# Three 32-byte offsets and the last operations of a streaming-encoder trunk

## The chip, the cores and the metric

The kernel runs on one core of one Trainium2 chip. The metric is the device time of one execution in microseconds (us). Times of several runs are given as a median; the trace is that of one profiled execution, whose own time stands beside its span below.

## What is computed

One layer of a trunk over 512 tokens of width 1024, all in float32. Four parallel mixers (a spatially gated MLP, gated linear attention, chunked attention, a convolution module) read one normalised input; each is projected and gated, and their sum is projected and added to the stream. A squared-ReLU MLP of width 4096 follows, and then the part which the tail of the kernel computes:

```python
def rms_norm(x, g):
    xf = x.astype(jnp.float32)
    y = xf * lax.rsqrt(jnp.mean(xf * xf, axis=-1, keepdims=True) + EPS)
    return (y * g.astype(jnp.float32)).astype(x.dtype)
...
        hg = rms_norm(h, norm3_g[i])
        ple_gate = jax.nn.sigmoid(jnp.einsum('bsd,de->bse', hg, w_ple_gate[i]) + b_ple_gate[i])
        h = h + ple_gate * jnp.einsum('bsq,qd->bsd', p[i], w_ple[i])
    return rms_norm(h, final_g)
```

The last norm has two factors for each element: one for its token (the reciprocal root, `rms` below) and one for its channel (`final_g`, `rowp[2]` and `rowp[3]` below).

## The kernel before

**Matmuls.** Every matrix product is written as three float32r products: each operand is split into a high and a low part (ScalarE copies the high part, VectorE subtracts), and high by high, low by high and high by low are added in PSUM. Weights come in pieces of 128 x 1024 numbers (`raw`, and `grow` for sums of pieces), are split into `wh` and `wl` (line 173 and 186 through `split_piece`), and are used by `ch_mm`, `tok_mm` or `product`, which all go through `mm` (line 191). One matmul reads a moving operand of 512 columns, while the next one's stationary operand of 128 columns is loaded. In the profile's names `b<-x,wh` the moving tile stands first and the stationary one second.

**Where tiles lie.** The order of all engines' work is the order of the program's text (`manual_schedule`). Memory of a partition is given out by pools that are stacked one behind the other. In a pool, a name with several buffers takes that many slots, in order of first use, and each slot is rounded up to 32 bytes. Pool `sb` is first and stays to the end. It begins at byte 16512, which is 0 modulo 64: `ident`, `later`, `jp`, `mean` (512 bytes each), `ind` (8 bytes, a slot of 32), `ones` (4, a slot of 32), `mhalf` (64), `vecs` (784 bytes, a slot of 800, which is 32 modulo 64). So everything that follows, from byte 19488 on, lies at 32 modulo 64 (and 32 modulo 128): `h`, `raw`, `wh`, `wl`, `x`, `v`, in slots that are multiples of 256 bytes together with the small ones between them. `sq3` (32 bytes) is asked for late, is the last of the pool, and brings its end to 133696, which is 0 modulo 64 (64 modulo 128). There the second pool begins: `early` (the tiles `u`, `stack`, `pad0` to `pad3`), and in its place later `late` (`grow`, `ht`, `act`, `combo`, `z`, `s1`, `s3`). All their tiles lie at 0 modulo 64. The `x`, `h`, `wh` and `wl` which matmuls read lie below byte 126240, and all tiles of the second pool above 133696.

Which pairs a matmul reads: input projections and gates read `x` with `wh`/`wl` (one pool). The first projections (up to 62 us), the branch products of three of the mixers and the output projection read `u` with `wh`/`wl` (two pools). The second half of the MLP reads `combo` with `wh`/`wl` (two pools), and its first half `x` (one pool). The attention scores read `stack` with `stack` (one pool, the second).

**The tail.** `ht[tb, half]` holds the stream: four blocks of 128 tokens, two halves of 512 channels. `gate(tb, half, b)` is one VectorE operation on the PSUM bank (norm factor, bias) and a tanh on ScalarE. `embed(tb, half)` is two VectorE operations (gate times embedding, then half of it added to `ht`) and a Square with a sum on ScalarE; `add_sum` (one small VectorE operation) adds its sum to the token's mean. `power` (line 369) raises to the power -0.5 on GpSimd. For each block, `first_part` lets GpSimd multiply half 0 by `rowp[2]` (line 1238), the evacuation lets GpSimd multiply half 1 by `rowp[3]` (line 1285), and `write` multiplies both halves by `rms[tb]`, on ScalarE (line 186) or for the later blocks on VectorE (line 182), and sends each half from the SP queue (line 1248). TensorE runs the second half's products block by block (24 matmuls of 512 columns); block 3 comes as two groups of 256 columns. The evacuation of block tb stands, in each engine's order, behind the products of block tb and ahead of the evacuation of block tb + 1.

Of the kernel before, what the change touches and what calls it, by code (L numbers as in the profile page):

```python
# [41 lines left out]
FILL = 0.72  # L42
WARM = 4
E_SLOTS = 28

# [83 lines left out]
def build(tc, x, w, vec, wa2, sgw, rows, rb, pt, out):  # L131
# [15 lines left out]
    def U(dt=F32):  # L147
        return epool.tile([128, 512], dt, tag="u", bufs=E_SLOTS, name=name("u"))

# [29 lines left out]
    def ts(o, a, s1, s2, op0, op1=None):  # L179
        cost["dve"] += 60 + 0.55 * size(o)  # L180
        if op1 is None:
            return DVE.tensor_scalar(o, a, s1, None, op0=op0)
        return DVE.tensor_scalar(o, a, s1, s2, op0=op0, op1=op1)  # L183

    def copy(o, a, **k):
        return ACT.activation(o, a, AF.Copy, **k)  # L186
# [34 lines left out]
    ones = gpool.tile([128, 1], F32, name="ones")  # L221
    mhalf = gpool.tile([128, 16], F32, name="mhalf")
    vecs = gpool.tile([128, NVEC], F32, name="vecs")
    warm = U()


# [84 lines left out]
    def step(last, mms, evac, own=True, lead=LEAD):  # L311

        prefetch(last, 0)
        now[0] = (last, lead)
        advance()
        b = bank() if own else None
        mms(b)
        fill()
        if evac is not None:
            evac(b)  # L320
        return b
# [36 lines left out]
    def tok_mm(o, j, i, tb, xk, nw, first, last, c0=0, cn=None):  # L358

        hi, lo = parts[j]  # L360
        c = slice(i * nw + c0, i * nw + c0 + (cn or nw))
        t = slice(tb * 128, tb * 128 + 128)
        mm(o, xk[0][:, t], hi[:, c], first, False)
        mm(o, xk[0][:, t], lo[:, c], False, False)
        mm(o, xk[1][:, t], hi[:, c], False, last)

    def power(ms, n):
        r = small(n)
        POOL.tensor_tensor(r, ms, mhalf[:, :n], op=OP.pow)  # L369
        return r  # L370
# [453 lines left out]
    for m in range(2):  # L824
        def evac(b):
            t = H()
            copy(t, b, scale=0.125)
            gq.append(t)
# [332 lines left out]
            transpose(b[:, tb * 128:tb * 128 + 128], ht[tb, k // 4][:, (k % 4) * 128:(k % 4) * 128 + 128])  # L1161
        hg3[k] = scaled_split(b, col("n3", k))

    sq3 = gpool.tile([128, 2, 4], F32, name="sq3")

    def squares(half):
        for tb in range(4):
# [48 lines left out]
    def gate(tb, half, b, c=slice(0, 512)):  # L1216
        z = zs[tb, half] = zt[half][:, tb, c]
        stt(z, b[:, c], rn["n3"][:, tb:tb + 1], rowp[half][:, c], OP.mult, OP.add)
        ACT.activation(z, z, AF.Tanh, scale=0.5)

    def embed(tb, half, c=slice(0, 512)):

        z = zs.pop((tb, half))
        stt(z, z, 1.0, ups[tb, half][:, c], OP.add, OP.mult)
        h = ht[tb, half][:, c]
        stt(h, z, 0.5, h, OP.mult, OP.add)
        a = small(1)
        ACT.activation(z, h, AF.Square, accum_out=a)  # L1228
        return a

    def add_sum(tb, a):
        e = small(1)
        ts(e, a, 1.0 / D, sums.get(tb, EPS), OP.mult, OP.add)
        sums[tb] = e

    def first_part(tb):
        a = embed(tb, 0)
        POOL.tensor_tensor(ht[tb, 0], ht[tb, 0], rowp[2], op=OP.mult)  # L1238
        add_sum(tb, a)

    def write(tb):
        for i in (1, 0):
            o = ht[tb, i]
            if i and tb >= 2:
                ts(o, o, rms[tb], None, OP.mult)
            else:
                copy(o, o, scale=rms[tb])
            nc.sync.dma_start(out[0, tb * 128:tb * 128 + 128, i * 512:i * 512 + 512], o)

    rms = {}  # L1250
    late_k = (4, 5, 6, 7, 0, 1, 2, 3)

    def channels():
# [7 lines left out]
    for i in range(4):  # L1261
        def mms(_, i=i):
            for q in range(2):
                if q:
                    middle()
                for tb in range(4):
                    tok_mm(bs[tb], base["ple0"] + i, q, tb, hg3[late_k[2 * i + q]], 512, i + q == 0, i + q == 4 and q == 1)

        step(base["ple0"] + i, mms, None, own=False, lead=4)
    for tb in range(4):  # L1270
        gate(tb, 0, bs[tb])
    first_part(0)
    for tb in range(4):
        def mms(b, tb=tb):
            for k in range(NKD):
                tok_mm(b, base["ple1"] + k // 2, k % 2, tb, hg3[late_k[k]], 512, k == 0, k == NKD - 1)

        def evac(b, tb=tb):
            gate(tb, 1, b)
            if tb:  # L1280
                write(tb - 1)
            first_part(tb + 1)
            add_sum(tb, embed(tb, 1))
            rms[tb] = power(sums[tb], 1)
            POOL.tensor_tensor(ht[tb, 1], ht[tb, 1], rowp[3], op=OP.mult)  # L1285

        if tb < 3:
            step(base["ple1"] + 3, mms, evac)
    for c in (0, 256):
        b = bank()  # L1290
        for k in range(NKD):
            tok_mm(b[:, c:c + 256], base["ple1"] + k // 2, k % 2, 3, hg3[late_k[k]], 512, k == 0, k == NKD - 1, c,
                   256)
        cs = slice(c, c + 256)
        gate(3, 1, b, cs)
        if c:
            write(2)
            tt(ht[3, 1][:, 0:256], ht[3, 1][:, 0:256], rowp[3][:, 0:256], OP.mult)
        add_sum(3, embed(3, 1, cs))
    rms[3] = power(sums[3], 1)  # L1300
    tt(ht[3, 1][:, 256:512], ht[3, 1][:, 256:512], rowp[3][:, 256:512], OP.mult)
    write(3)
    ctx.close()


# [60 lines left out]
```

## Time and profile before

| | us |
|---|---|
| median of 3 runs | 1006.32 (1005.86 to 1007.16) |
| the profiled execution's own time | 1004.86 |
| its span in the trace | 1002.9 |
| TensorE busy in the span | 981.5 (98%) |
| VectorE busy | 661.6 (66%) |
| ScalarE busy | 412.0 (41%) |
| GpSimd busy | 86.7 (9%) |

The span runs from the first to the last recorded instruction; the own time has 1.96 us around it. TensorE's matmuls are pipelined: the profile models their ends, so that two neighbours overlap, and what counts is the time from one start to the next. In a row that merges n instructions, start to start is (the row's length less the length of one) divided by n - 1. "Idle before" is time in which an engine had nothing to run, with what ended it.

### The profile page before, as it was taken

How to read it: one execution, taken by the hardware profiler on the slowest of the kernel's cores; microseconds unless marked ns; L12 is line 12 of the kernel's file. 1: busy time of each engine (PE TensorE's matmuls, PEld its weight loads, DVE VectorE, ACT ScalarE, POOL GpSimd, SP SyncE). 2: the span in 40 equal slices, each digit the busy share in tenths (PEclk: the TensorE clock that was granted, in tenths of full speed). 3: DMA queues.
4: the chain of work that ended last, by engine and by line, in shares of the span. 5: the costliest groups of instructions: out<-in, count | busy, mean ns of one | idle time of the engine just before them, and what ended most of it. 6: DMA issues, size and time to landing. Idle time of an engine off the chain costs nothing.

```text
span 1002.9 us, 11777 instructions
## 1 busy us (share of the span) xinstructions
PE 981.5 (98%) x4550; PEld 805.9 (80%) x4550; DVE 661.6 (66%) x917; ACT 412.0 (41%) x615; POOL 86.7 (9%) x94
## 2 busy tenths in 40 slices
PE   8999999999999999999999999999999999999993
PEld 6978888887888888888888888888888888877882
DVE  7746896487888987555444543575575587578565
ACT  6554764223323232324333434444434334335633
POOL 5001000001001500000000000020011011001012
PEclk9999999999999999999999999999999999999997
DMA  6334331322242223223252242464566459568202
GB/s 237 129 109 141 97 95 64 106 96 73 92 144 101 98 74 123 65 83 126 90 171 96 84 147 70 120 141 132 168 149 187 126 151 232 168 152 221 84 1 84
DMA packets 36595, 121.02 MB, mean 121 GB/s; under 512 B 4123, under 2 KB 4284, under 8 KB 36540
## 3 DMA queue, kind: packets, MB, share of 16 engines
q1 hardware_dynamic: 31292, 101.40, 30.2%
q0 software_dynamic: 5248, 18.88, 10.2%
q8 instruction: 36, 0.59, 0.2%
q14 instruction: 19, 0.16, 0.0%
HBM read 116.07 MB, written 2.10 MB: 118 GB/s over the span
## 4 chain that ended last, share of the span: by engine, by line
PE 92%; DVE 3%; issue 2%; ACT 1%; POOL 1%; DMA 1%; SPq 0%; POOLq 0%; DVEq 0%; ACTq 0%
PE b L191 90%; PE b L195 2%; DVE wl L173 1%; DVE ht L173 1%; DMA stack<-stack 0%; POOL ht L1285 0%; DMA raw<-w 0%; DVE s L173 0%; ACT ht L186 0%; ACT combo L186 0%; DVE z L177 0%; ACT z L1228 0%; POOL ht L1238 0%; POOL s L369 0%; DVE ht L177 0%
## 5 line engine op out<-in xcount | busy, mean ns | idle before, releaser
L191 PE MATMUL b<-x,wh 128*128 128x512 f32 x1440 | 361.2, 392 | 0.0
L191 PEld LDWEIGHTS b<-x,wh 128*128 128x128 f32 x1440 | 267.9, 188 | 56.7 <-issue 1.2
L173 DVE TENSOR_TENSOR wl<-raw,wh 128x1024 fp32r<-128x1024 f32 (+2 forms) x166 | 202.5, 1235 | 47.8 <-ACT wh L186 46.6
L191 PE MATMUL b<-x,wl 128*128 128x512 f32 x720 | 192.8, 389 | 0.0
L186 ACT ACTIVATE wh<-raw 128x1024 fp32r<-128x1024 f32 (+2 forms) x166 | 169.3, 1041 | 24.7 <-PE b L191 19.5
L191 PEld LDWEIGHTS b<-x,wl 128*128 128x128 f32 x720 | 135.2, 188 | 28.2
L191 PE MATMUL b<-wh,combo 128*128 128x512 f32 x448 | 144.5, 396 | 0.5 <-DVE ht L173 0.5
L191 PEld LDWEIGHTS b<-wh,combo 128*128 128x128 f32 x448 | 84.1, 188 | 20.7 <-issue 0.9
L191 PE MATMUL b<-wl,combo 128*128 128x512 f32 x224 | 88.8, 397 | 0.3 <-DVE wl L173 0.3
L177 DVE SCALAR_TENSOR_TENSOR u<-pad,vecs,u 128x512 f32<-128x512 f32 x120 | 86.2, 780 | 0.0
L191 PE MATMUL b<-u,wh 128*128 128x512 f32 x320 | 85.4, 396 | 0.0
L1005 ACT ACTIVATE act<-act 128x512 f32<-128x512 f32 x32 | 20.2, 633 | 150.9 <-DVE act L177 150.9
L191 PEld LDWEIGHTS b<-u,wh 128*128 128x128 f32 x320 | 59.8, 188 | 14.5 <-issue 0.3
L177 DVE SCALAR_TENSOR_TENSOR u<-u,b 128x512 f32<-128x512 f32 x36 | 24.7, 685 | 68.7 <-PE b L191 64.3
L191 PE MATMUL b<-wh,x 128*128 128x512 f32 (+1 forms) x208 | 60.8, 374 | 0.0
L857 ACT ACTIVATE u<-b,vecs 128x512 f32<-128x512 f32 x32 | 22.0, 686 | 90.3 <-PE b L191 90.3
L177 DVE SCALAR_TENSOR_TENSOR act<-b,v 128x512 f32<-128x512 f32 x32 | 22.0, 691 | 55.8 <-PE b L191 55.4
L191 PE MATMUL b<-wh,u 128*128 128x512 f32 (+1 forms) x192 | 53.5, 362 | 1.2 <-ACT wh L186 1.2
L369 POOL TENSOR_TENSOR s<-s,mhalf 128x4 f32<-128x4 f32 (+1 forms) x16 | 15.4, 965 | 441.7 <-DVE s L183 321.6
L191 PEld LDWEIGHTS b<-wl,combo 128*128 128x128 f32 x224 | 42.1, 188 | 11.4 <-DVE wl L173 1.5
L191 PE MATMUL b<-u,wl 128*128 128x512 f32 x160 | 47.7, 395 | 0.0
L191 PEld LDWEIGHTS b<-wh,x 128*128 128x128 f32 x208 | 38.1, 188 | 6.9
(171 smaller groups left out, 1029.7 us busy)
## 6 DMA issues: line engine op xcount, KB each, us to landing
raw<-w SPq DMA_DIRECT2D x161, 512.0 KB, 3.4
grow<-w POOLq DMA_DIRECT2D x24, 512.0 KB, 7.8
h<-x SPq DMA_DIRECT2D x16, 256.0 KB, 5.2
grow<-w SPq DMA_DIRECT2D x8, 512.0 KB, 4.7
raw<-w POOLq DMA_DIRECT2D x8, 512.0 KB, 6.9
v<-rb SPq DMA_DIRECT2D x8, 256.0 KB, 4.3
stack<-stack POOLq DMA_DIRECT2D x8, 256.0 KB, 3.8
out<-ht SPq DMA_DIRECT2D x8, 256.0 KB, 2.1
```

The lines of the kernel that those rows point to most:

```text
L173: return DVE.tensor_tensor(o, a, b, op=op)
L177: return DVE.scalar_tensor_tensor(o, a, s, b, op0=op0, op1=op1)
L186: return ACT.activation(o, a, AF.Copy, **k)
L191: PE.matmul(o, l, r, start=start, stop=stop, **k)
L195: PE.transpose(o, i, ident)
L369: POOL.tensor_tensor(r, ms, mhalf[:, :n], op=OP.pow)
L857: ACT.activation(th, gb, AF.Tanh, scale=0.5, bias=col("bg", n * 8 + m))
L1005: ACT.activation(a, a, AF.Square)
```

## The change

Two tiles of pool `sb` are asked for right behind `vecs`: `sq3`, which was the pool's last, and a new `pad` of 32 bytes that nothing uses. With `sq3` behind `vecs` the next byte is 0 modulo 64, with the pad 32 modulo 64: the large tiles of `sb` now begin at 19552, and the pool ends at 133728. Both are 32 modulo 64 (and 96 modulo 128), so all tiles of all pools that matmuls read have one offset.

In the tail no product by `rowp` is left on GpSimd. For blocks 0 to 2, `finish` multiplies by the token's factor and by the channel's in one VectorE operation and sends. For block 3, `gained` multiplies half 0 and the first 256 columns of half 1 by the channel's factor on VectorE ahead of the sum, ScalarE multiplies these by the token's, and the last 256 columns go through the one VectorE operation. The embedding of half 0 of block tb + 1 moves ahead of the evacuation of block tb, and the power stands right behind the last sum. Both 256-column groups of block 3 stand, in TensorE's order, ahead of all evacuation of block 3. There are nine output transfers in place of eight.

```diff
--- before.py
+++ after.py
@@ -42,6 +42,7 @@
 FILL = 0.72
 WARM = 4
 E_SLOTS = 28
+PAD = 8
 
 
 
@@ -221,6 +222,8 @@
     ones = gpool.tile([128, 1], F32, name="ones")
     mhalf = gpool.tile([128, 16], F32, name="mhalf")
     vecs = gpool.tile([128, NVEC], F32, name="vecs")
+    sq3 = gpool.tile([128, 2, 4], F32, name="sq3")
+    gpool.tile([128, PAD], F32, name="pad")
     warm = U()
 
 
@@ -1161,7 +1164,6 @@
             transpose(b[:, tb * 128:tb * 128 + 128], ht[tb, k // 4][:, (k % 4) * 128:(k % 4) * 128 + 128])
         hg3[k] = scaled_split(b, col("n3", k))
 
-    sq3 = gpool.tile([128, 2, 4], F32, name="sq3")
 
     def squares(half):
         for tb in range(4):
@@ -1228,26 +1230,30 @@
         ACT.activation(z, h, AF.Square, accum_out=a)
         return a
 
-    def add_sum(tb, a):
+    rms = {}
+
+    def add_sum(tb, a, last=False):
         e = small(1)
         ts(e, a, 1.0 / D, sums.get(tb, EPS), OP.mult, OP.add)
         sums[tb] = e
-
-    def first_part(tb):
-        a = embed(tb, 0)
-        POOL.tensor_tensor(ht[tb, 0], ht[tb, 0], rowp[2], op=OP.mult)
-        add_sum(tb, a)
-
-    def write(tb):
-        for i in (1, 0):
-            o = ht[tb, i]
-            if i and tb >= 2:
-                ts(o, o, rms[tb], None, OP.mult)
-            else:
-                copy(o, o, scale=rms[tb])
-            nc.sync.dma_start(out[0, tb * 128:tb * 128 + 128, i * 512:i * 512 + 512], o)
-
-    rms = {}
+        if last:
+            rms[tb] = power(e, 1)
+
+    def send(tb, half, c):
+        nc.sync.dma_start(out[0, tb * 128:tb * 128 + 128, half * 512 + c.start:half * 512 + c.stop], ht[tb, half][:, c])
+
+    def gained(tb, half, c=slice(0, 512)):
+        tt(ht[tb, half][:, c], ht[tb, half][:, c], rowp[2 + half][:, c], OP.mult)
+
+    def finish(tb, half, c=slice(0, 512), gain=True):
+
+        o = ht[tb, half][:, c]
+        if gain:
+            stt(o, o, rms[tb], rowp[2 + half][:, c], OP.mult, OP.mult)
+        else:
+            copy(o, o, scale=rms[tb])
+        send(tb, half, c)
+
     late_k = (4, 5, 6, 7, 0, 1, 2, 3)
 
     def channels():
@@ -1269,37 +1275,50 @@
         step(base["ple0"] + i, mms, None, own=False, lead=4)
     for tb in range(4):
         gate(tb, 0, bs[tb])
-    first_part(0)
-    for tb in range(4):
-        def mms(b, tb=tb):
-            for k in range(NKD):
-                tok_mm(b, base["ple1"] + k // 2, k % 2, tb, hg3[late_k[k]], 512, k == 0, k == NKD - 1)
-
+    sq = {}
+
+    def second(tb, b, c0=0, cn=512):
+        for k in range(NKD):
+            if cn == 512 and k == NKD // 2:
+                middle()
+            tok_mm(b[:, c0:c0 + cn], base["ple1"] + k // 2, k % 2, tb, hg3[late_k[k]], 512, k == 0, k == NKD - 1, c0, cn)
+
+    for tb in range(3):
         def evac(b, tb=tb):
+            if tb == 0:
+                sq[0, 0] = embed(0, 0)
+                sq[1, 0] = embed(1, 0)
+            else:
+                add_sum(tb - 1, sq.pop((tb - 1, 0)))
+                a = embed(tb - 1, 1)
+                sq[tb + 1, 0] = embed(tb + 1, 0)
+                add_sum(tb - 1, a, True)
             gate(tb, 1, b)
             if tb:
-                write(tb - 1)
-            first_part(tb + 1)
-            add_sum(tb, embed(tb, 1))
-            rms[tb] = power(sums[tb], 1)
-            POOL.tensor_tensor(ht[tb, 1], ht[tb, 1], rowp[3], op=OP.mult)
-
-        if tb < 3:
-            step(base["ple1"] + 3, mms, evac)
-    for c in (0, 256):
-        b = bank()
-        for k in range(NKD):
-            tok_mm(b[:, c:c + 256], base["ple1"] + k // 2, k % 2, 3, hg3[late_k[k]], 512, k == 0, k == NKD - 1, c,
-                   256)
-        cs = slice(c, c + 256)
-        gate(3, 1, b, cs)
-        if c:
-            write(2)
-            tt(ht[3, 1][:, 0:256], ht[3, 1][:, 0:256], rowp[3][:, 0:256], OP.mult)
-        add_sum(3, embed(3, 1, cs))
-    rms[3] = power(sums[3], 1)
-    tt(ht[3, 1][:, 256:512], ht[3, 1][:, 256:512], rowp[3][:, 256:512], OP.mult)
-    write(3)
+                finish(tb - 1, 0)
+                finish(tb - 1, 1)
+
+        step(base["ple1"] + 3, lambda b, tb=tb: second(tb, b), evac)
+    cs = [slice(0, 256), slice(256, 512)]
+    bs = [bank(), bank()]
+    second(3, bs[0], 0, 256)
+    second(3, bs[1], 256, 256)
+    add_sum(2, sq.pop((2, 0)))
+    a = embed(2, 1)
+    add_sum(3, sq.pop((3, 0)))
+    gained(3, 0)
+    add_sum(2, a, True)
+    gate(3, 1, bs[0], cs[0])
+    finish(2, 0)
+    a = embed(3, 1, cs[0])
+    finish(2, 1)
+    add_sum(3, a)
+    gained(3, 1, cs[0])
+    gate(3, 1, bs[1], cs[1])
+    add_sum(3, embed(3, 1, cs[1]), True)
+    finish(3, 0, gain=False)
+    finish(3, 1, cs[1])
+    finish(3, 1, cs[0], gain=False)
     ctx.close()
```

## Rows read from the trace of the kernel before

**Rows 1.** Page, part 4: chain that ended last, shares of the span by engine.

```profile
PE 92%; DVE 3%; issue 2%; ACT 1%; POOL 1%; DMA 1%; SPq 0%; POOLq 0%; DVEq 0%; ACTq 0%
```

**Rows 2.** Timeline, TensorE: start us, length us, what, merged count.

```profile
204.18 3.34 PE L191 MATMUL b<-x,wh 128*128 128x512 f32 x14
...
549.78 3.43 PE L191 MATMUL b<-u,wh 128*128 128x512 f32 x14
...
800.94 0.63 PE L191 MATMUL b<-wh,combo 128*128 128x512 f32 x2
```

**Rows 3.** Groups by form, TensorE, whole span: count | busy us, mean ns | idle before.

```profile
L191 PE MATMUL b<-x,wh 128*128 128x512 f32 x1440 | 361.2, 392 | 0.0
...
L191 PE MATMUL b<-x,wl 128*128 128x512 f32 x720 | 192.8, 389 | 0.0
...
L191 PE MATMUL b<-wh,combo 128*128 128x512 f32 x448 | 144.5, 396 | 0.5 <-DVE ht L173 0.5
...
L191 PE MATMUL b<-wl,combo 128*128 128x512 f32 x224 | 88.8, 397 | 0.3 <-DVE wl L173 0.3
...
L191 PE MATMUL b<-u,wh 128*128 128x512 f32 x320 | 85.4, 396 | 0.0
...
L191 PE MATMUL b<-u,wl 128*128 128x512 f32 x160 | 47.7, 395 | 0.0
...
L191 PE MATMUL b<-wh,u 128*128 128x512 f32 x128 | 41.4, 398 | 1.2 <-ACT wh L186 1.2
...
L191 PE MATMUL b<-wl,u 128*128 128x512 f32 x64 | 25.4, 397 | 0.2 <-DVE wl L173 0.2
```

**Rows 4.** Timeline, TensorE, narrower products of two pools.

```profile
31.32 0.42 PE L191 MATMUL b<-wh,u 128*128 128x272 f32 x2
```

**Rows 5.** Timeline, TensorE, attention scores: both operands in the second pool.

```profile
99.97 0.62 PE L191 MATMUL b<-stack,stack 128*128 128x512 f32 x2
...
100.42 0.51 PE L191 MATMUL b<-stack,stack 128*128 128x384 f32 x2
```

**Rows 6.** Timeline, TensorE: one-pool products right behind two-pool ones.

```profile
245.71 3.37 PE L191 MATMUL b<-x,wh 128*128 128x512 f32 x14
```

**Rows 7.** Windows: length, busy us of PE, PEld, DVE, ACT, POOL; clock; DMA.

```profile
880.60:909.40 28.80, 28.12 (x121) 22.11 (x119) 24.68 (x28) 12.35 (x13) 4.71 (x6) 1.00 0.60 141
```

**Rows 8.** Timeline, TensorE: its last matmul.

```profile
985.09 0.28 PE L191 MATMUL b<-wh,x 128*128 128x256 f32 x1
```

**Rows 9.** Output tensor's transfers on SP: issue ns min/median/max, first and last start.

```profile
L1248 SPq DMA_DIRECT2D out<-ht x8: 332/333/384, 978.5 to 999.3; - x8
```

**Rows 10.** Timeline, VectorE in the tail.

```profile
969.45 0.68 DVE L177 SCALAR_TENSOR_TENSOR z<-z,act 128x512 f32<-128x512 f32 x1
970.17 0.69 DVE L177 SCALAR_TENSOR_TENSOR ht<-z,ht 128x512 f32<-128x512 f32 x1
...
971.72 1.81 DVE L177 SCALAR_TENSOR_TENSOR z<-z,act 128x512 f32<-128x512 f32 x1
...
975.18 0.74 DVE L177 SCALAR_TENSOR_TENSOR z<-b,s,h 128x512 f32<-128x512 f32 x1
975.84 0.68 DVE L177 SCALAR_TENSOR_TENSOR z<-z,act 128x512 f32<-128x512 f32 x1
...
995.90 0.42 DVE L177 SCALAR_TENSOR_TENSOR z<-z,act 128x256 f32<-128x256 f32 x1
996.36 0.42 DVE L177 SCALAR_TENSOR_TENSOR ht<-z,ht 128x256 f32<-128x256 f32 x1
997.42 0.21 DVE L183 TENSOR_SCALAR s<-s,s 128x1 f32<-128x1 f32 x1 [0.64 <-ACT z L1228]
```

**Rows 11.** Timeline, GpSimd in the tail.

```profile
971.69 1.29 POOL L1238 TENSOR_TENSOR ht<-ht,h 128x512 f32<-128x512 f32 x1 [4.15 <-ACT z L1228]
```

**Rows 12.** Timeline, ScalarE: its last instruction.

```profile
998.40 0.72 ACT L186 ACTIVATE ht<-ht,s 128x512 f32<-128x512 f32 x1 [1.01 <-POOL s L369]
```

**Rows 13.** Groups by form, VectorE: two tiles and a factor per partition.

```profile
L177 DVE SCALAR_TENSOR_TENSOR u<-h,vecs,u 128x512 f32<-128x512 f32 x8 | 5.6, 747 | 0.0
```

## The prediction

> **What bounds the kernel now.** The shares of the chain that ended last come first: TensorE carries 92% of it and VectorE 3% [rows 1]. So a saving counts where TensorE's matmuls come closer together, or behind its last matmul. That one ends at 985.09 + 0.28 = 985.37 us [rows 8], and the last output transfer is issued at 999.3 [rows 9]: 13.9 us in which TensorE does nothing. The change touches both places.
>
> Next is TensorE's timeline inside long runs without any idle time, where the distance from start to start can be worked out. Fourteen matmuls that read `x` and `wh`, both from pool `sb`, take 3.34 us; less the last one's 0.39 that is 2.95 for 13 steps, 227 ns. Fourteen of the same form that read `u` and `wh`, from two pools, take 3.43: 3.035 for 13 steps, 233.5 ns. A `combo` pair takes 0.63 less 0.395, 235 ns [rows 2]. The reader is to see that nothing waits in these runs, that form and clock are the same, and that the pair of pools alone goes with 6.6 ns more. It is long both where the second pool's tile is the moving operand (`u`) and where it is the stationary one (`combo`).
>
> **Part 1, the offsets.** By the sizes in the code the tiles of `sb` lie at 32 modulo 64 now and those of the second pool at 0; afterwards all lie at 32. The pad and the earlier `sq3` add no instruction. If the long step comes from unequal offsets, each two-pool step of 512 columns falls from 233.3 to 226.7. Their count: 448 + 224 + 320 + 160 + 128 + 64 = 1344 [rows 3]. 1344 x 6.6 ns = 8.9 us. The narrower two-pool matmuls give nothing: at 272 columns one step is 0.42 - 0.29 = 0.13 us [rows 4], and 272 columns at 2.4 GHz are 0.113, so they already carry the same 13 ns over the bare columns as the short step does (227 - 213).
>
> Two corrections. After a two-pool run, a one-pool run takes 3.37 in place of 3.34 [rows 6, 2], as if it had to settle; the code changes back from two pools to one some 45 times (24 times in three mixers' branches, the rest around the MLP's products). That is 0.03 x 45 = 1.4 us at most; I take 0.5, since many of these changes also have transposes between them that disturb the run anyway. Against that, from 880.6 to 909.4 VectorE is busy 24.7 of 28.8 us [rows 7], with sums, splits and evacuations that wait on each other; 96 of the 1344 matmuls lie there, and I count their 0.6 us as lost to VectorE (between nothing lost and all of it; TensorE, at 28.1 of 28.8 us, has little idle time there yet). Elsewhere TensorE shows next to no idle time ahead of these groups (2.2 us in all, [rows 3]), so the feeding engines have slack of a size that the rows don't show; a TensorE that is 3% faster in these runs may use some of it up, up to 0.8 us more. Part 1: 8.9 + 0.5 - 0.6 = 8.8 us, with bounds 7.4 and 10.3.
>
> Here the Trainium skill speaks against the change. "TensorE: Matmul & The Clock Gate", section "Step-by-step: what each phase is for", says that loading the next tile's weights doesn't steal read bandwidth from the running matmul, since TensorE has two independent read ports. By it, where the tiles lie could not matter, and part 1 would be 0. The trace shows two lengths of step for the same form, so something the page doesn't tell is at work; whether it is the offset is what rival A asks.
>
> **Part 2, the tail.** Removed: seven products by `rowp` on GpSimd. They cost VectorE more than GpSimd: an embedding's first step takes 0.68 alone and 1.81 beside GpSimd's product of 1.29 that began 0.03 before it [rows 10, 11]. Removed also: the second multiplication by `rms`, on ScalarE or VectorE. Added on VectorE: one operation for each half of blocks 0 to 2, of a kind (two tiles and a factor per partition) that takes 0.75, from 0.66 by the spacing of the gates to 0.75 as it stands [rows 10, 13]; I take 0.7. For block 3 two products by `rowp` of 0.7 and 0.4.
>
> I follow VectorE's order in the changed text against the old clock of TensorE (part 1 shifts both alike). Prices from start to start: gate 0.66 (975.18 to 975.84), embedding 0.72 + 0.70 (969.45, 970.17), at 256 columns 0.46 + 0.46 (995.90, 996.36), small ones 0.1 to 0.2 [rows 10]. TensorE ends block 2 some 5.7 us ahead of its end, at 979.65: two groups of 24 half-width steps of 0.12 (256 columns at 2.4 GHz, 0.107, and the 13 ns). Block 2's gate, two finishes, a small one and its second embedding's two steps wait only for VectorE itself and for a tanh that the two finishes cover:
> - gate 980.3, finishes of block 1 981.0 and 981.7, embedding 983.2;
> - small, product by `rowp` for block 3, small: 984.2;
> - gate of block 3's first half-width group, 0.45 by the same estimate, 984.65; first finish of block 2 waits for the power (0.98 from the sum to its use: 997.42 to 998.40 [rows 10, 12]) until 985.0, ends 985.7;
> - embedding at 256 columns 986.6, second finish 987.3, small and product 987.9;
> - gate of the last group 988.4 (its matmuls ended at 985.37, so here VectorE, not TensorE, sets the time), tanh 0.45 (an estimate: as long as an embedding step of that width), embedding 989.8;
> - Square and its sum 0.64 [rows 10], power 0.98: 991.4; copy 0.72 [rows 12]: 992.1; its transfer is issued 0.2 later (999.12 to 999.3 before), and two more at 0.33 each [rows 9] follow: the last starts at 993.0.
>
> 993.0 against 999.3: 6.3 us. That the blocks don't queue up earlier is to be seen in one block's VectorE work: gate 0.66, two finishes 1.4, two embeddings 2.84, two or three small ones 0.4, together 5.3, under the 24 x 0.227 = 5.4 of its matmuls. That is the narrow place: at 0.75 for a finish, with the small waits between, it is 5.5 or so and adds 0.1 for each of two blocks. The ninth transfer costs its 0.33, counted above; the halved ones may land a little sooner or later than the 256 KB ones, which I set at 0. Bounds: 5.0 (each of the twelve operations of the list 0.1 us longer) and 7.0 (finishes at 0.66, gates of half width at 0.4).
>
> **Sum.** 8.8 + 6.3 = 15.1 us. The profiled execution would fall from 1004.86 to 989.8 (span 1002.9 to 987.8). It lies 1.46 us below the median of the runs shown, and I take that distance as kept: 1006.32 - 15.1 = 991.2 us. With the bounds 12.4 and 17.3 the forecast's own range is 989.0 to 993.9.
>
> **The rivals.** A: the offset modulo 64 is not the cause. The second pool's tiles differ in another thing: all lie above byte 133696, while the tiles of `sb` that matmuls read end below 126240. If a long step comes from operands that lie far apart, or on two sides of some boundary in the memory, nothing moves, since the pools stay where they are. Then only part 2 is left: 1006.3 - 6.3 = 1000.0. For it: the trace has no pair of unequal offsets inside one pool, so the two readings can't be parted by it. Against it: a short step also after the second pool has been entered by both operands, and a step that doesn't grow with the distance (`u` begins 60 KB above `wh`, `combo` 100 KB, and both have 6.6 ns). The skill's sentence on two independent ports would give the same time. 11%.
>
> B, the other side: what is short is not equality but the place itself, 32 modulo 128, where all of `sb` lies now. Afterwards every tile lies at 96 modulo 128, and all steps may become long: the 1440 + 720 steps with `x` as the moving operand [rows 3] x 6.6 ns are 14.3 us more, less the tail's 6.3: 1014.3. It decides against the change from 6.3 / 0.0066 = 950 lengthened steps on. Against it: `stack` with `stack`, both at 64 modulo 128, goes from 99.97 to 100.42 for two matmuls, 225 ns each [rows 5], the short step; but such pairs are few, and one of two. 5%.
>
> C: the offsets do what they say, and the tail gives nothing, because VectorE takes over GpSimd's products and the blocks queue behind it. Of the 5.3 us a block, 1.4 us are new; if each of the six finishes took 1.8 us, as an operation with two tiles does beside GpSimd now [rows 10], that would be 6 x 1.1 = 6.6 us more, and the tail's gain were gone. But no product is left on GpSimd to stand beside; only one power of one column for each block is. 1006.3 - 8.8 = 997.5. 4%.
>
> **How the numbers follow.** Forecast 80%, A 11%, B 5%, C 4%. The range reaches from the forecast's lower bound, 989.0, up to C's 997.5; what is left out are A, B and a little of the forecast's own edges, 2 in 10. About 0.2% (2 us) is what a measurement of this kernel can tell from no change: forecast, A and C are all faster by more, 94%; B slower, 5%; 1% for an A whose tail fails too.
>
> **What would show it.** Right: runs of 14 matmuls of `u` take 3.34 in place of 3.43, groups of 512 columns with `u` and `combo` have a mean near 390 ns in place of 396; no rows of GpSimd on `ht`, no embedding step over 1.1 us; TensorE's last matmul near 976.6; from it to the last issue 7.6 us in place of 13.9. Wrong: `u` and `combo` still at 396 (A), `x` at 396 (B), or VectorE's gates in the tail later and later behind TensorE's blocks (C). If the groups are short and the span still isn't near 988, TensorE has new idle time in front of `wh` or `wl`, and the cover that I took for granted was thin.

## The result, and the profile after

| | before | after |
|---|---|---|
| median of the runs beside each other, us | 1006.17 (4 runs) | 990.45 (989.06 to 990.62, 4 runs) |
| ratio, 95% interval | | 0.9839 (0.9822 to 0.9856) |
| the profiled execution's own time, us | 1004.86 | 990.44 |
| its span, us | 1002.9 | 988.7 |

The forecast was 991.2. In after.py the lines are shifted: `mm` is line 192, the copy on ScalarE 187, VectorE's operations 174, 178 and 184, `power` 372, tanh 1221, Square 1230, the output's transfer 1243.

**The chain** of after (page, part 4: shares of the span by engine) is what [rows 1] are for before: TensorE carries 95% in place of 92%, all others together 5%.

```profile
PE 95%; DVE 2%; issue 1%; ACT 1%; DMA 0%; SPq 0%; POOLq 0%; POOL 0%; ACTq 0%; DVEq 0%
```

**TensorE's timeline** of after (start us, length us, what, merged count, idle time before and its releaser):

```profile
6.52 0.80 PE L192 MATMUL b<-wh,u 128*128 128x512 f32 x1 [1.29 <-ACT wh L187]
...
7.84 1.05 PE L192 MATMUL b<-wh,u 128*128 128x512 f32 x2
...
9.12 1.05 PE L192 MATMUL b<-wh,u 128*128 128x512 f32 x2
...
10.40 0.78 PE L192 MATMUL b<-wh,u 128*128 128x512 f32 x2
...
246.08 3.34 PE L192 MATMUL b<-x,wh 128*128 128x512 f32 x14
...
542.14 3.33 PE L192 MATMUL b<-u,wh 128*128 128x512 f32 x14
...
781.74 0.62 PE L192 MATMUL b<-wh,combo 128*128 128x512 f32 x2
...
894.07 0.50 PE L192 MATMUL b<-wl,combo 128*128 128x512 f32 x1 [0.87 <-DVE wl L174]
...
902.84 0.47 PE L192 MATMUL b<-wh,combo 128*128 128x512 f32 x1 [0.51 <-DVE ht L174]
...
978.07 0.28 PE L192 MATMUL b<-wh,x 128*128 128x256 f32 x1
```

Four things are to be seen. A run of fourteen with `u` takes 3.33 where it took 3.43 [rows 2]: (3.33 - 0.39) / 13 = 226 ns a step. A run of `x` right behind two-pool work takes 3.34 where it took 3.37 [rows 6]: nothing is left to settle. The last matmul starts 7.02 us earlier [rows 8]. And from 7.84 to 10.40 two matmuls and the one behind them take 1.28, 427 ns a step: 512 columns at 1.2 GHz. The granted clock in the profile's rows reads 1.00 from 7.0 to 10.4 us all the same, so here the lower level is read from the steps alone. In the profile of before the same matmuls have short steps:

```profile
7.46 0.62 PE L191 MATMUL b<-wh,u 128*128 128x512 f32 x2
...
8.15 0.63 PE L191 MATMUL b<-wh,u 128*128 128x512 f32 x2
```

0.69 for three steps is 230 ns. So after's profiled execution lost some 1.6 us in its first 11 us that before's didn't lose, and the offsets' gain has to be read from behind that.

**The groups by form** of after (count | busy us, mean ns | idle before), beside [rows 3]:

```profile
L192 PE MATMUL b<-x,wh 128*128 128x512 f32 x1440 | 360.5, 391 | 0.0
...
L192 PE MATMUL b<-wh,combo 128*128 128x512 f32 x448 | 141.8, 390 | 0.5 <-DVE ht L174 0.5
L192 PE MATMUL b<-wl,combo 128*128 128x512 f32 x224 | 87.5, 391 | 0.9 <-DVE wl L174 0.9
L192 PE MATMUL b<-u,wh 128*128 128x512 f32 x320 | 83.3, 390 | 0.0
...
L192 PE MATMUL b<-u,wl 128*128 128x512 f32 x160 | 46.7, 389 | 0.0
L192 PE MATMUL b<-wh,u 128*128 128x512 f32 x128 | 42.1, 404 | 1.3 <-ACT wh L187 1.3
...
L192 PE MATMUL b<-wl,u 128*128 128x512 f32 x64 | 25.8, 404 | 0.0
```

`combo` and `u` fell from 396 to 390, and `x` stayed. Only the two groups of the first microseconds (`wh,u` and `wl,u`) rose, to 404, by the low clock there. The idle time of TensorE ahead of `wl` went from 0.3 to 0.9.

**The tail** of after: the output's transfers on SP (issue ns min/median/max, first and last start), then VectorE's timeline.

```profile
L1243 SPq DMA_DIRECT2D out<-ht x9: 332/332/404, 968.6 to 985.5; - x9
```

```profile
967.87 1.41 DVE L178 SCALAR_TENSOR_TENSOR ht<-ht,s,h 128x512 f32<-128x512 f32 x2
...
974.69 0.68 DVE L178 SCALAR_TENSOR_TENSOR z<-z,act 128x512 f32<-128x512 f32 x1
...
977.02 0.47 DVE L178 SCALAR_TENSOR_TENSOR z<-b,s,h 128x256 f32<-128x256 f32 x1
977.82 0.75 DVE L178 SCALAR_TENSOR_TENSOR ht<-ht,s,h 128x512 f32<-128x512 f32 x1 [0.33 <-POOL s L372]
...
978.94 0.43 DVE L178 SCALAR_TENSOR_TENSOR ht<-z,ht 128x256 f32<-128x256 f32 x1
979.28 0.75 DVE L178 SCALAR_TENSOR_TENSOR ht<-ht,s,h 128x512 f32<-128x512 f32 x1
...
980.47 0.48 DVE L178 SCALAR_TENSOR_TENSOR z<-b,s,h 128x256 f32<-128x256 f32 x1
...
982.95 0.21 DVE L184 TENSOR_SCALAR s<-s,s 128x1 f32<-128x1 f32 x1 [0.64 <-ACT z L1230]
```

From the start of the last matmul to the last issue it is 985.47 - 978.07 = 7.40 us, where it was 999.34 - 985.09 = 14.24 [rows 8, 9]: 6.84 less. Two finishes together take 1.41, so 0.66 from one to the next, and an embedding's first step takes 0.68 everywhere, never the 1.81 beside GpSimd [rows 10].

### The profile page after: what moved, and what is told of

Its sections match the earlier page's. It is cut to its first block, busy times and chain, and to the rows that moved or that the text cites. A ratio compares the mean times of both kernels' runs of the same rounds, so it can differ in the third digit from the quotient of the medians.

```text
span 988.7 us, 11769 instructions
## 1 busy us (share of the span) xinstructions
PE 974.1 (99%) x4550; PEld 807.2 (82%) x4550; DVE 659.0 (67%) x922; ACT 409.4 (41%) x611; POOL 76.8 (8%) x87
## 3 DMA queue, kind: packets, MB, share of 16 engines
q0 software_dynamic: 5248, 18.88, 10.4%
## 4 chain that ended last, share of the span: by engine, by line
PE 95%; DVE 2%; issue 1%; ACT 1%; DMA 0%; SPq 0%; POOLq 0%; POOL 0%; ACTq 0%; DVEq 0%
PE b L192 93%; PE b L196 2%; DVE wl L174 1%; DVE ht L174 1%; DMA raw<-w 0%; DVE s L174 0%; ACT combo L187 0%; DVE ht L178 0%; DVE z L178 0%; DVE combo L174 0%; ACT z L1230 0%; ACT ht L187 0%; DVE act L178 0%; ACT act L1008 0%; ACT wh L187 0%
## 5 line engine op out<-in xcount | busy, mean ns | idle before, releaser
L192 PE MATMUL b<-wh,combo 128*128 128x512 f32 x448 | 141.8, 390 | 0.5 <-DVE ht L174 0.5
L192 PE MATMUL b<-u,wh 128*128 128x512 f32 x320 | 83.3, 390 | 0.0
```

What stands on the lines that cost most here:

```text
L192: PE.matmul(o, l, r, start=start, stop=stop, **k)
```

## The experiments

The theory: steps of 512 columns are long where the two operands' addresses don't match, the change makes them match, and the tail falls by what VectorE's order allows. The rivals are those of the prediction. A median stands with its number of runs; before, beside them, is at 1005.78 (9 runs) for the first four kernels, 1005.87 (7) for the next four and 1005.49 (9) for the last four.

**One part alone: offsets only.** The tail of before with the memory layout of after.

```diff
+    sq3 = gpool.tile([128, 2, 4], F32, name="sq3")
+    gpool.tile([128, PAD], F32, name="pad")
     warm = U()
...
-    sq3 = gpool.tile([128, 2, 4], F32, name="sq3")
```

> The kernel before with the offsets of the change alone (sq3 and the pad behind vecs, the old tail). Theory: the offsets are worth what TensorE gained between the two traces; from 85 us on its clock time fell by 7.6 us, and the two-pool steps ahead of that are worth about 1 us more, so 1006.2 - 8.6 = 997.6 us, between 996.5 and 999, with u and combo groups at a mean of 390 ns and the last issue still 13.9 us behind TensorE's end. Rival (the tail's new order is what shortened the steps, for instance by its other allocation): 1006 us and groups at 396 ns.

996.88 us (4 runs), ratio 0.9911 (0.9895 to 0.9928). Its groups with `combo`, and those with `u` as the moving tile, are those of after to the nanosecond. Its clock was up as early as before's, so spans can be compared: 1002.9 to 994.9, 8.0 us, and the last matmul starts 8.04 earlier. The tail stays at 14.24. Rival A, by which the offsets give nothing, is out.

**The other part alone: tail only.** after.py without the two lines above and with `sq3` back in its place.

> The changed kernel with sq3 back at its late place and without the pad: the new tail on the old offsets. Theory: only the tail's 6.7 us are left, 1006.2 - 6.7 = 999.5 us, between 998.5 and 1000.5, groups of u and combo at 396 ns. Rival (what two parts gain is not a sum: with a faster TensorE the tail gains less or more): the gains of this run and of the one with the offsets alone add up to something else than 15.7 us by over 1 us.

997.27 us (4 runs), ratio 0.992 (0.9905 to 0.9935). `u` and `combo` are at 396, the tail at 7.40; the span falls from 1002.9 to 995.5, 7.4 us. With 8.0 for the offsets that makes 15.4. The time lies below the expected range: 999.5 was taken from a before of 1006.2, and this profile's own time, 997.27, has to be set against a before whose clock was up early too (1004.86). By medians the two parts gain 8.9 and 8.5, together 17.4, and both at once 15.7; a median can hold runs with the clock up early and late, which is 1.6 us (below), so the rival, that the parts don't add up, is judged by the spans: 15.4 here, and 15.8 for both at once with the clock early (1002.9 less 987.1).

**Equality or the place: no pad.** after.py without `pad`, so that the pools lie at 0 modulo 64 and not at 32.

```diff
-    gpool.tile([128, PAD], F32, name="pad")
```

> The changed kernel without the pad, sq3 still early: all large tiles of both pools at 0 modulo 64 (64 modulo 128). Theory (equal offsets are what counts): 990.5 us, all groups at 390 ns. Rival (the place counts, 32 modulo 64 is the good one): every step of 512 columns long, 3912 x 6.6 ns = 26 us more, 1016 us; if 0 is the better place, faster than 990.

990.1 us (4 runs), ratio 0.9844 (0.9829 to 0.9858); `u` and `combo` at 389 to 391. The place doesn't count, which rival B needed. The pad isn't needed either: `sq3` moved behind `vecs` is enough.

**Unequal inside one pool: `x` apart.** after.py with 32 bytes in front of `x`, and 32 more at the pool's end, so that `x` lies 32 bytes off `wh`, and the second pool 64 bytes further.

```diff
+        if not xpad:
+            xpad.append(gpool.tile([128, 8], F32, name="xpad"))
...
+    gpool.tile([128, 8], F32, name="endpad")
```

> The changed kernel with 32 unused bytes ahead of x inside pool sb and 32 at the pool's end: x lies at 0 modulo 64, wh, wl and the second pool at 32. Pairs of x with wh or wl are now unequal inside one pool, in neighbouring memory. Theory: these 1440 + 720 + 176 + 88 = 2424 steps become long, 2424 x 6.6 ns = 16 us: 1006.5 us, groups of x at 396 ns, of u and combo at 390. Rival A (distance or the side of byte 131072 counts): x stays at 390 ns and the time at 990.5.

1009.18 us (4 runs), ratio 1.0034 (1.0018 to 1.0049). Groups by form of this kernel:

```profile
L196 PE MATMUL b<-x,wh 128*128 128x512 f32 x1440 | 368.6, 397 | 0.0
L196 PE MATMUL b<-x,wl 128*128 128x512 f32 x720 | 197.1, 395 | 0.0
L196 PE MATMUL b<-wh,combo 128*128 128x512 f32 x448 | 144.4, 396 | 0.5 <-DVE ht L178 0.5
...
L196 PE MATMUL b<-u,wh 128*128 128x512 f32 x320 | 83.9, 392 | 0.0
```

`x` with `wh`, neighbours in one pool, went from 391 to 397. Pools and sides of a boundary are out; the offset alone makes the step long. But `combo` was expected short, since it is equal modulo 64 with `wh`, and is at 396; `u` as the moving tile is between, at 392. Equality modulo 64 can't be the condition.

**Which distances are short: 27 of them.** after.py, with each `combo` tile of the MLP's second half, the stationary operand there, begun so many bytes further on in a slot made longer. Each distance has one product of 24 matmuls (48 has two).

```diff
-        t = lpool.tile([128, 2, 4, 256], F32R, tag="combo", bufs=4, name=name("combo"))
+        whole = lpool.tile([128, 2112], F32R, tag="combo", bufs=4, name=name("combo"))
+        i = 7 * g + ("a11", "a12", "s1", "s2", "s3", "s4", "n22").index(n)
+        off = 4 * i if i < 16 else (1, 2, 3, 5, 6, 7, 9, 10, 11, 12, 14, 15)[i - 16]
+        t = whole[:, off:off + 2048].rearrange("p (q k n) -> p q k n", q=2, k=4)
```

> The changed kernel with each of the 28 combo tiles (the stationary operand of one product of 48 matmuls) moved by its own distance inside a wider slot: 0, 16, 32, ... 240 bytes for the first 16, and 4, 8, 12, 20, 24, 28, 36, 40, 44, 48, 56, 60 bytes for the rest; the moving operand stays. Theory 64 (equal modulo 64): short steps (227 ns) at 0, 64, 128 and 192 bytes, long ones at 32. Theory 128, since the run with x apart showed long combo steps where combo and wh differed by 64: short at 0 and 128 alone. Theory 256: short at 0 alone. Between these distances no theory here has a number; a step that falls below 227 ns anywhere would be a better offset than equality.

992.91 us (one run). The timeline of TensorE, from products 16, 64 and 144 bytes off (start us, length us):

```profile
645.45 0.39 PE L192 MATMUL b<-wl,combo 128*128 128x512 f32 x1
...
646.13 0.39 PE L192 MATMUL b<-wl,combo 128*128 128x512 f32 x1
...
689.30 0.39 PE L192 MATMUL b<-wl,combo 128*128 128x512 f32 x1
...
690.00 0.40 PE L192 MATMUL b<-wl,combo 128*128 128x512 f32 x1
...
739.12 0.39 PE L192 MATMUL b<-wl,combo 128*128 128x512 f32 x1
...
739.80 0.39 PE L192 MATMUL b<-wl,combo 128*128 128x512 f32 x1
```

From one of these to the next it is three steps: 0.68 at 16 and 144 bytes, 0.70 at 64. The mean step of each product, worked out from the start times:

| bytes off | mean step, ns |
|---|---|
| 0, 12, 16, 144, 240 | 226.6 to 227.7 |
| 8, 24, 44, 60, 176, 192 | 229.0 to 231.2 |
| 4, 20, 28, 32, 36, 40, 48, 56, 64, 80, 96, 112, 128, 160, 208, 224 | 231.8 to 235.1 |

Zero is short, and so are a few others; 32, 64 and 128 are not. By the sizes in the code (the trace has no addresses), all large tiles of after lie a multiple of 256 bytes apart. In before the second pool was 32 off. Why 12, 16, 144 and 240 are short as well isn't settled: each is one product, and its slot differs too.

**Moved by 64: the second pool.** after.py with 64 bytes at the end of pool `sb`.

```diff
+    gpool.tile([128, 16], F32, name="pad64")
```

> The changed kernel with 64 unused bytes at the end of pool sb: the second pool stays equal to sb modulo 64, and differs by 64 modulo 128. Theory 64: as the changed kernel, 990.3 us, u and combo at 390 ns. Theory 128 or 256: combo and the early u at 396 ns again, u as the moving operand in the branches between 390 and 396 (it had 392 in the run with x apart): 3.1 + 1.2 + 1.1 + about 0.8 us, so 996.5 us.

996.62 us (2 runs), ratio 0.991. Groups by form:

```profile
L192 PE MATMUL b<-wh,combo 128*128 128x512 f32 x448 | 144.5, 396 | 0.5 <-DVE ht L174 0.5
...
L192 PE MATMUL b<-u,wh 128*128 128x512 f32 x320 | 84.3, 393 | 0.0
```

All offsets are equal modulo 64 here, and `combo` is long throughout, so equality modulo 64 isn't what the change works by. Its pools lie at equal places modulo 256, and that is short in every kernel here that has it.

`u` as the moving tile is long in part only, and the table says why if the distance is taken with its sign, as the place of the stationary tile less that of the moving one. `combo` is the stationary one and lies 64 further: the table's 64, long. Where `u` moves, the same two pools give -64, which is 192 modulo 256: the table's 229.0, and the steps of `u,wh` and `u,wl` are 230.0 and 229.1 here, 228.7 and 229.5 with `x` apart. Where `u` is stationary, in the first projections, it is +64 again, and the steps of `wh,u` are 233.3 in both kernels. Before fits too: 32 for `combo` and -32, that is 224, for a moving `u`, both long in the table. That 256 is the period rests on these signs alone. Why some distances are long isn't known.

**GpSimd off, all else as before: the tail's first share.** The offsets-only kernel with the products by `rowp` on VectorE.

```diff
-        POOL.tensor_tensor(ht[tb, 0], ht[tb, 0], rowp[2], op=OP.mult)
+        tt(ht[tb, 0], ht[tb, 0], rowp[2], OP.mult)
...
-            POOL.tensor_tensor(ht[tb, 1], ht[tb, 1], rowp[3], op=OP.mult)
+            tt(ht[tb, 1], ht[tb, 1], rowp[3], OP.mult)
```

> The run with the offsets alone, and in its old tail the seven products by rowp moved from GpSimd to VectorE, nothing else. Theory (GpSimd beside VectorE is what the old tail paid for): no embedding step over 0.8 us; VectorE takes 7 x 0.69 us more and saves about 1.0 for each of some seven lengthened steps, and the power no longer stands ahead of a product on GpSimd; the tail from TensorE's end to the last issue falls from 14.2 to about 11.5 us, 994 us. Rival (order is what counts): the tail stays within 0.7 us of 14.2, 996.9 us, since VectorE's work grows as much as it gets faster.

994.48 us (4 runs). The last matmul's start to the last issue is 11.21 in place of 14.24: taking the products off GpSimd gives 3.0 us.

**Both factors in one operation, in the old order.** after.py, with each embedding and its sum back behind the gate and the finishes. The diff is cut: the lines that these two replace, and block 3, where the first group's gate and embedding go back ahead of the second group's products and block 2's finishes ahead of the last embedding.

```diff
             if tb:
                 finish(tb - 1, 0)
                 finish(tb - 1, 1)
+            add_sum(tb + 1, embed(tb + 1, 0))
+            add_sum(tb, embed(tb, 1), True)
...
```

> The changed kernel with the one operation for both factors and the nine transfers kept, but the embedding of the next block's half 0 and the last block's evacuation back in the old order (gate of this block, writing of the last one, then both embeddings). Theory: order is worth what is left after GpSimd, some 2 us of the tail's 6.8: 992.3 us, tail 9.5 us. Rival: the order gives nothing, VectorE has the same work either way, 990.3 us.

994.02 us (4 runs), ratio 0.9884 (0.9869 to 0.9899). The tail is 11.88, not 9.5, and 0.67 longer than the 11.21 with GpSimd off, which has the old order and two operations. That isn't the one operation alone. Block 3's second gate, first with GpSimd off (last matmul at 977.44), then in this kernel (at 977.92):

```profile
984.10 0.48 DVE L178 SCALAR_TENSOR_TENSOR z<-b,s,h 128x256 f32<-128x256 f32 x1
```

```profile
983.72 0.47 DVE L178 SCALAR_TENSOR_TENSOR z<-b,s,h 128x256 f32<-128x256 f32 x1
```

It begins 6.66 us behind the last matmul's start there and 5.80 here, so up to this point the kernel with one operation is 0.86 ahead. It loses that behind the gate: from there to the last small sum it is 3.56 us in place of 2.63, with both finishes of block 2 on VectorE in between where the other has one multiplication, and the ninth transfer is issued 0.48 behind the eighth. VectorE's timeline of this kernel:

```profile
978.05 0.15 DVE L184 TENSOR_SCALAR s<-s 128x1 f32<-128x1 f32 x1 [0.85 <-ACT z L1230]
...
980.38 0.21 DVE L184 TENSOR_SCALAR s<-s,s 128x1 f32<-128x1 f32 x1 [0.85 <-ACT z L1230]
```

With each sum right behind its embedding, VectorE stands idle 0.8 us for ScalarE's Square, twice a block. The new order puts the next embedding there. The new order as a whole is worth 11.88 - 7.40 = 4.5 of the tail's 6.84.

**The clock at the start: six warming matmuls, and after once more.** after.py with `WARM = 6`, beside after.py itself.

> The kernel after, with six instead of four of the matmuls on memset data that run ahead of the first real one (in the profile of after eight records, 1.45 to 5.23 us; the first real matmul starts at 6.52). Theory: TensorE's clock rises late in this kernel (steps of 427 ns until 10.4 us) in most runs, because TensorE is idle for 1.29 us ahead of the first real matmul, and that costs about 1.6 us; with two more the idle time is gone, the 427 ns steps are gone, and the median is about 989.0, while the first real matmul starts up to 0.6 us later, near 7.1. Rival: the idle time has nothing to do with when the clock rises; then the steps of 427 ns stay in the profile and the time is 990.3 to 990.8.

> The kernel after, unchanged, beside the three others on the same chip. Theory: 990.3 median, with single runs between 988.8 (clock up early) and 990.8 (late). Rival: a median within 0.3 us of the kernel with six warming matmuls, which would say that the early matmuls decide nothing.

988.9 us (988.69 to 989.18, 4 runs) and, for after again, 989.19 (988.86 to 990.22, 4 runs; ratio 0.9837, 0.9824 to 0.9851). TensorE's timeline of the kernel with six, then of after again:

```profile
6.17 0.50 PE L192 MATMUL b<-wh,u 128*128 128x512 f32 x1 [0.39 <-ACT wh L187]
...
7.24 0.64 PE L192 MATMUL b<-wh,u 128*128 128x512 f32 x2
```

```profile
6.12 0.49 PE L192 MATMUL b<-wh,u 128*128 128x512 f32 x1 [1.13 <-ACT wh L187]
...
7.17 0.63 PE L192 MATMUL b<-wh,u 128*128 128x512 f32 x2
```

Its clock is up early, as the theory had it. But this time after's own profile has it early too, behind 1.13 us without work, and the medians are 0.3 us apart, as the rival had it. So the idle time ahead of the first real matmul doesn't make the clock late by itself, and what does is open. The other traces say the same. With four warming matmuls six of eleven have some seven steps of 427 ns at the start, behind idle times of 0.65 (GpSimd off) to 1.53 us (no pad), and five have none, behind 0.93 (moved by 64) to 1.28 us (tail only). The three with six warming matmuls have none, which three traces can't tell from chance. What the pair does show is the price: after again starts its last matmul at 976.51 where the first profile had 978.07. That is 1.56 us, as far apart as the own times, 988.86 and 990.44, and at 97 us the two profiles already lie 1.60 apart.

**The wait for `wl`: split first.** The kernel with six, with the next slot's split ahead of the running generator's steps in the last group of products.

```diff
+        if late_split[0]:
+            prefetch(*now[0])
+            advance("mid")
+        else:
+            advance("mid")
+            prefetch(*now[0])
```

> The previous kernel with one more edit: in the last group of products (the stretch 860 to 915 us) the split of the next weight slot is put on VectorE ahead of the steps of the running generator, instead of behind them. Theory: TensorE's wait for wl at 892.8 us in after (0.87 us idle, released by VectorE) goes, and with it some 0.8 us: about 988.2 if the previous kernel is at 989.0. Rival: VectorE has too much work in this stretch in any order, and the wait only moves to the operands that the generator makes (s, x tiles): no change, 989.0.

991.36 us (990.72 to 991.89, 4 runs): 2.5 us slower, where a gain of 0.8 or none was expected. The timeline of VectorE, then the wait of TensorE that follows:

```profile
899.42 2.36 DVE L174 TENSOR_TENSOR wl<-grow,wh 128x1024 fp32r<-128x1024 f32 x2 [2.07 <-ACT wh L187]
901.70 1.22 DVE L174 TENSOR_TENSOR combo<-s,combo 128x1024 fp32r<-128x1024 f32 x1
902.84 1.27 DVE L174 TENSOR_TENSOR ht<-ht,b 128x512 f32<-128x512 f32 x2
...
903.66 0.47 PE L192 MATMUL b<-wh,combo 128*128 128x512 f32 x1 [2.64 <-DVE ht L174]
```

The split stands ahead of `combo` now and waits 2.07 us for ScalarE's high part. `combo` and the evacuation into `ht` queue behind it on VectorE, and the evacuation is what TensorE waits for. The wait for `wl` near 892 shrank only from 0.88 to 0.66. Neither theory nor rival had this.

**Another order in the tail.** The kernel just told, with block 3's second gate and embedding ahead of block 2's finishes.

```diff
     gate(3, 1, bs[0], cs[0])
-    finish(2, 0)
     a = embed(3, 1, cs[0])
-    finish(2, 1)
+    gate(3, 1, bs[1], cs[1])
+    finish(2, 0)
+    c = embed(3, 1, cs[1])
     add_sum(3, a)
     gained(3, 1, cs[0])
-    gate(3, 1, bs[1], cs[1])
-    add_sum(3, embed(3, 1, cs[1]), True)
+    add_sum(3, c, True)
+    finish(2, 1)
```

> The previous kernel with one more edit, in the tail behind TensorE's last matmul: block 3's second gate goes to VectorE as soon as the second quarter is in, and the two finishing operations of block 2 (0.75 us each) are moved into the waits for tanh and for power. In after the second gate starts 2.40 us behind the start of the last matmul, though the quarter is in after 0.3 us, and the two finishes and 0.42 us of gain stand between. Theory: last issue at about 6.0 to 6.2 us behind the last matmul's start instead of 7.40: about 1.2 us less, 987.0 if the previous kernel is at 988.2. Rival: the chain gate, tanh, two operations, Square, sum, power, finish is bound elsewhere (the order only moves the waits for ScalarE): no change, 988.2.

990.56 us (989.86 to 990.71, 5 runs), 0.8 less than the kernel that it was made from. The last matmul's start to the last issue is 6.24 in place of 7.40. Timeline of this kernel, TensorE's last matmul, VectorE and GpSimd:

```profile
979.35 0.28 PE L192 MATMUL b<-wh,x 128*128 128x256 f32 x1
...
980.06 0.48 DVE L178 SCALAR_TENSOR_TENSOR z<-b,s,h 128x256 f32<-128x256 f32 x1
...
982.76 0.74 DVE L178 SCALAR_TENSOR_TENSOR ht<-ht,s,h 128x512 f32<-128x512 f32 x1
...
982.92 0.98 POOL L378 TENSOR_TENSOR s<-s,mhalf 128x1 f32<-128x1 f32 x1 [3.86 <-DVE s L184]
```

The last gate starts 0.71 behind the last matmul's start in place of 2.40. The tail is 1.16 shorter; the span fell by 0.9 only, because the last matmul starts 0.20 later than in the kernel before (979.35 against 979.15). In this profile TensorE ran at 427 ns a step for 3 us near 903 (last section). Without the split's order this edit would give some 988.0 (989.2 less 1.2), which wasn't run. Of the kernels that ran, none is measurably faster than after.

## Why the prediction held, and where its terms were off

**The sum.** With the clock early in both profiles, before's own time of 1004.86 stands against 988.86 of after again: 16.0 us. The prediction's sum was 15.1. The first profile of after, with its clock late, gives 14.4. The forecast of 991.2 had no term for that, in either direction. So it lies 0.75 from the first median and 2.0 from the second (989.19), and that it came so near the first is partly luck. The 16.0 is 8.58 up to the last matmul, 6.84 from there to the last issue, 0.4 behind that and 0.2 outside the span.

**Part 1, 8.8.** Like for like, the last matmul starts 985.09 - 976.51 = 8.58 us earlier; the offsets alone gave 8.04. The 0.54 between them lies ahead of 97 us, where after again starts its first real matmul 0.2 earlier; behind it both gain 7.5. The count of 1344 and the 6.6 ns held: the groups fell by 6 to 7 ns [rows 3]. Summing all distances from start to start, what the two-pool steps take over the short step fell from 8.66 to 0.45 us, so 8.2 of the 8.9. The settling, taken at 0.5 of at most 1.4, was 1.0 (one-pool steps: 1.8 to 0.8). The stretch in which VectorE sets the pace was taken at 0.6, and TensorE's idle time ahead of `wl` grew there from 0.3 to 0.87 (the row at 894.07), by some 0.55, while the wait at 902.84 was there before with 0.5 [rows 3]. That new idle time in front of `wh` or `wl` would mean thin cover stands in the prediction; it came at this one place. The lower bound of part 1 comes to 7.5 from its own terms, not 7.4; nothing hangs on that.

**Modulo 64.** Here the prediction was right for a reason that doesn't hold, which is luck. It took over "unequal modulo 64" from the sizes, and noted the places modulo 128 only for rival B. The kernels with `combo` 64 bytes off show that equal modulo 64 is long as well. Before could not show it: its one unequal distance is 32. A pad that made the pools equal modulo 64 and 64 apart modulo 128 would have passed the same argument, and given 996.6. That the place modulo 256 came out equal too wasn't asked for.

**The Trainium skill's sentence** on two independent read ports ("TensorE: Matmul & The Clock Gate", "Step-by-step: what each phase is for"), which spoke against part 1, doesn't cover these runs: with the same form and clock, a step takes 227 or 233 ns by the address distance of the moving tile and the weights loaded beside it. Whether the two reads take time from each other, or the distance acts in another way, no run shows.

**Part 2, 6.3.** Measured 6.84, inside 5.0 to 7.0. But the terms named for the upper bound don't reach it: four finishes in the list shorter by 0.04 and two gates by 0.05 make 0.26, so 6.6, and the measured gain lies above that. Counted from the last matmul's start, the prediction has the last gate begin 2.8 behind it and the last issue 7.9; after has 2.40 and 7.40. So nearly all of the difference lies ahead of the last gate. Half of it is between block 2's first finish and that gate, 2.65 in place of 2.9: a finish takes 0.66 to the next start and not 0.7, and an embedding's last step at 256 columns 0.34 (978.94 to 979.28) and not 0.46. Behind the gate the list held to 0.1. The transfers, set at 0, gave some 0.4: from the last issue to the span's end 3.58 us fell to 3.20.

Where that gain comes from, the prediction left in one list, and the expectation for the old order shows that it wasn't understood: it took the order to be worth some 2 and the one operation to be a gain. The runs give 3.0 for GpSimd, -0.7 for the one operation with its ninth transfer and old order in block 3, and 4.5 for the order. What was missed is VectorE's wait for Square. Before's timeline has it, twice a block, and [rows 10] show it only once, as the 0.64 at 997.42:

```profile
979.69 0.15 DVE L183 TENSOR_SCALAR s<-s 128x1 f32<-128x1 f32 x1 [1.47 <-ACT z L1228]
...
983.15 0.21 DVE L183 TENSOR_SCALAR s<-s,s 128x1 f32<-128x1 f32 x1 [0.85 <-ACT z L1228]
```

The prediction counted 5.3 us of VectorE's operations a block against TensorE's 5.4. That leaves no room for some 1.6 us of waits a block, so the list came out only because the changed order covers them, a condition that the prediction doesn't name.

VectorE's 1.81 beside GpSimd falls under "SBUF — State Buffer", "Who interferes with whom", of the Trainium skill: an operation of VectorE with two inputs in SBUF contends with a GpSimd instruction that reads SBUF. The trace agrees, with 0.68 for the same operation once GpSimd is off, and in the other direction with `power` at 0.98 beside a finish and 0.54 without one.

**The rivals.** A fell with the offsets alone (8.0 us) and with `x` apart; B with the kernel without the pad; C with the tail's 6.84. `x` apart is B's price come true in another way (B had counted only the 2160 with a moving `x`): 2424 steps with `x` and 1344 others lengthened (480 of them, with a moving `u`, by 2 to 3 ns), and slower than before.

## What to carry to other kernels

Where two long runs of one form have different steps, work out the addresses of both operands and move one by a few bytes: here 8.0 us of 1005, 0.8%, hung on a tile of 32 bytes. Test the rule as well as the change, with a second distance, before a layout is built on it. In a tail, follow the slowest engine's order instruction by instruction, and put work that is ready into each wait for another engine; an operation that is ready must not stand behind one that waits.

## What the runs showed of the chip

- A TensorE step of 512 columns in float32r takes 226.7 ns or some 233.3, by the distance in memory between the moving operand and the weights loaded beside it: short at 0 and at four others of 27 distances within 256 bytes, long at 32, 64 and 128, and between at six. Which of the two lies further counts: 64 is 233.3, -64 is 229 to 230.
- At the start of the same program TensorE's steps are 230 ns from the first real matmuls on in one execution (after again), and 427 ns until 10.4 us in another (the first profile of after). Over all traces the idle time ahead doesn't tell the two apart: 0.65 to 1.53 us where the short steps came late, 0 to 1.28 where they came early. That is 1.6 us of the whole, a tenth of what the change brings. The granted clock in the profile's rows reads 1.00 in both cases.
- In the last kernel TensorE idled 2.63 us at 900 us and then ran its steps at 427 ns for 3 us (granted clock 0.57 from 903 to 907); in the kernel before it the same idle of 2.64 us brought none of that.
